# DeltaNet's convolution and SiLU in a Trainium2 encoder step: per group of 384 tokens at the eviction of the projection, in place of per tile of 128 in the DeltaNet stage

## Chip, cores and metric

One Trainium2 chip, one NeuronCore of it. The metric is device time of one launch in microseconds (us). Times per instruction come from one profiled execution.

## What is computed

One layer of a streaming encoder for 2048 prompt tokens and 8 x 16 sample tokens (2176 tokens, 17 tiles of 128). One input projection feeds three token mixers: chunked band attention, gated DeltaNet, and an S5 state-space model (S5). Their outputs go through an output projection, a layer norm, a feed-forward network (FFN) and a second layer norm. The part that the change concerns is the head of DeltaNet:

```
buf = concat([conv_buf, qkv_b], axis=1)          # 3 earlier rows, then the projected 768 columns
new_conv = buf[:, -3:]
conv = depthwise causal convolution of width 4 over buf (768 channels)
conv = silu(conv + b_conv_b)
qb, kb, vb = split(conv, 3)
qb, kb = l2_normalize(qb), l2_normalize(kb)
ob, s_new = gated_delta_rule(qb, kb, vb, g, beta, s0)
```

For the prompt `conv_buf` is zero before the first token; for the 8 sample streams it is an input of 3 rows each.

## The kernel before

All features lie on partitions: the 768 q/k/v channels of DeltaNet are 6 blocks of 128 channels, called f = 0 to 5 here.

**Projection.** `project1` goes through the tokens in three parts of 768, 768 and 640 tokens, each part in two groups (384 and 384; in the last part 384 and 256, the 256 being 128 prompt tokens and the 128 sample tokens). For every part `feat` is called with blocks of 256 output columns: first S5's input, then `tok` for value columns and gates, then three `feat` calls for the q/k/v channels of DeltaNet, then one for DeltaNet's output gate. One `feat` call makes four PSUM tiles (2 halves of 128 columns x 2 groups), each from 8 x 3 matmuls, since a product of fp32 numbers is made of three products of split parts. The PSUM pool for them, `pp`, has 2 buffers. Each PSUM tile is evicted by ScalarE (`evac`, L198) into a tile of the pool `st` (2 buffers, `to_rows`), which SyncE's DMA queue (SP) then stores to the DRAM buffer `bT[part]`. `project2` and `project2_all` make the attention's q, k and v in the same way afterwards.

**DeltaNet.** `deltanet` takes the 17 tiles in pairs (0 1, 2 3, ... 10 11, then the sample tile 16, then 12 13, 14 15). `b_pre` loads a tile's six blocks from `bT` with three earlier columns (`cin`, 3 buffers, L499 to L505), and for each block does: on ScalarE the first tap with the bias (L510), on VectorE three taps (L512), on ScalarE a tanh (L514), on VectorE the closing product (L515; silu(x) is x(1 + tanh(x/2)) up to a factor that the later scales hold). The result `s2` (1 buffer) is transposed by TensorE (L528, L535). `b_inverse` inverts the 16x16 diagonal blocks on VectorE (L625, L627) with a round trip through DRAM, `b_solve` and `b_rec` are chains of small matmuls (L649, L686 to L694) and VectorE steps, `b_out` ends the tile.

**Order.** The two streams are Python generators. Part 0 is projected alone; from then on the emission alternates between DeltaNet and the projection of parts 1 and 2, and later between DeltaNet, `project2_all` and `s5`. A list scheduler then fixes the order in which each engine, and each DMA queue, gets its instructions. At run time an engine takes them strictly in that order, so an instruction that waits holds everything behind it on its engine. After this stage come attention, the output projection and the FFN.

## Time and profile before

| | us |
|---|---|
| median of 3 runs (2867.49 to 2869.89) | 2867.68 |
| the profiled execution, own time | 2862.88 |
| its span | 2861.1 |
| TensorE (PE) busy in the span | 2739.1 |
| VectorE (DVE) busy | 1945.7 |
| ScalarE (ACT) busy | 1316.4 |
| GpSimd (POOL) busy | 1096.7 |

In the rows below, PE is the matmul part of TensorE and PEld its weight loads. L512 is line 512 of the kernel before. "out<-in" names the tile that is written and the tiles that are read. "idle before" is the idle time of the engine just in front of an instruction, with what ended it. The chain of waits is followed back from the last instruction: at each step to what released it, or to the instruction in front of it on its engine.

### The profile page before, as it was taken

How to read it: one execution, taken by the hardware profiler on the slowest of the kernel's cores; microseconds unless marked ns; L12 is line 12 of the kernel's file. 1: busy time of each engine (PE TensorE's matmuls, PEld its weight loads, DVE VectorE, ACT ScalarE, POOL GpSimd, SP SyncE). 2: the span in 40 equal slices, each digit the busy share in tenths (PEclk: the TensorE clock that was granted, in tenths of full speed). 3: DMA queues.
4: the chain of work that ended last, by engine and by line, in shares of the span. 5: the costliest groups of instructions: out<-in, count | busy, mean ns of one | idle time of the engine just before them, and what ended most of it. 6: DMA issues, size and time to landing. Idle time of an engine off the chain costs nothing.

```text
span 2861.1 us, 46393 instructions
## 1 busy us (share of the span) xinstructions
PE 2739.1 (96%) x16685; PEld 2404.6 (84%) x16685; DVE 1945.7 (68%) x4908; ACT 1316.4 (46%) x2743; POOL 1096.7 (38%) x972
## 2 busy tenths in 40 slices
PE   8999999989989899999999999999999999999998
PEld 8988888867677677788889989979999898888897
DVE  7587888798653788778755555566665656566666
ACT  3554554343355778612334334354344345444443
POOL 0011111231221223002654444465555554677674
PEclk9999999999999999999999999999999999999999
DMA  5644445455457651244612212252222225322321
GB/s 184 208 107 119 115 121 127 137 150 151 152 156 247 204 160 57 92 148 162 240 63 80 68 60 74 74 206 104 74 89 89 74 79 201 112 89 89 118 83 58
DMA packets 292429, 351.89 MB, mean 123 GB/s; under 512 B 85586, under 2 KB 218534, under 8 KB 291878
## 3 DMA queue, kind: packets, MB, share of 16 engines
q1 hardware_dynamic: 292198, 348.92, 38.9%
q8 instruction: 131, 2.15, 0.3%
q14 instruction: 100, 0.82, 0.1%
HBM read 276.58 MB, written 74.89 MB: 123 GB/s over the span
## 4 chain that ended last, share of the span: by engine, by line
PE 70%; DVE 12%; POOL 5%; DMA 5%; ACT 4%; issue 4%; SPq 1%; DVEq 0%; ACTq 0%; POOLq 0%
PE fdp L66 7%; PE fdp L65 7%; PE fdp L67 7%; PE pps L66 3%; PE pps L67 3%; PE pps L65 3%; PE wops L66 2%; PE wops L65 2%; PE wops L67 2%; PE fupv L65 2%; PE fupv L66 2%; PE fupv L67 2%; PE fupz L67 2%; PE bqs L649 2%; PE fupz L66 2%
## 5 line engine op out<-in xcount | busy, mean ns | idle before, releaser
L1552 POOL TENSOR_TENSOR wu<-wur,wu 128x512 fp32r<-128x512 f32 x315 | 424.2, 1350 | 530.8 <-ACT wu L1551 512.2
L1670 DVE TENSOR_TENSOR fy<-fy,fdp 128x512 f32<-128x512 f32 x500 | 342.3, 687 | 271.8 <-PE fdp L67 270.2
L1551 ACT CAST wu<-wur 128x512 fp32r<-128x512 f32 x315 | 194.0, 617 | 450.8 <-DMA wur<-in_w_upL 203.5
L65 PE MATMUL fdp<-wdh,hh 128*128 128x512 f32 x1020 | 397.8, 390 | 2.4 <-DVE fy L1670 1.9
L66 PE MATMUL fdp<-wdl,hh 128*128 128x512 f32 x1020 | 397.3, 389 | 0.0
L67 PE MATMUL fdp<-wdh,hl 128*128 128x512 f32 x1020 | 397.1, 389 | 0.0
L65 PE MATMUL pps<-xh,wh 128*128 128x384 f32 (+2 forms) x800 | 279.5, 351 | 12.4 <-ACT xh L60 10.6
L66 PE MATMUL pps<-xl,wh 128*128 128x384 f32 (+2 forms) x800 | 279.6, 349 | 2.1 <-DVE xl L61 2.0
L67 PE MATMUL pps<-xh,wl 128*128 128x384 f32 (+2 forms) x800 | 277.4, 347 | 0.1
L65 PEld LDWEIGHTS fdp<-wdh,hh 128*128 128x128 f32 x1020 | 191.5, 188 | 42.5 <-DVE fy L1670 3.7
L1617 DVE TENSOR_TENSOR hl<-fre,hh 128x384 fp32r<-128x384 f32 (+1 forms) x180 | 162.9, 906 | 92.1 <-ACT hh L1616 91.3
L67 PEld LDWEIGHTS fdp<-wdh,hl 128*128 128x128 f32 x1020 | 191.5, 188 | 39.9
L66 PEld LDWEIGHTS fdp<-wdl,hh 128*128 128x128 f32 x1020 | 191.5, 188 | 38.0 <-DVE wdl L61 0.2
L60 ACT CAST wdh<-wdr 128x1024 fp32r<-128x1024 f32 x94 | 97.9, 1050 | 174.2 <-PE fdp L67 171.0
L65 PEld LDWEIGHTS pps<-xh,wh 128*128 128x128 f32 x800 | 152.0, 191 | 24.7 <-ACT xh L60 12.1
L61 DVE TENSOR_TENSOR wl<-wr,wh 128x512 fp32r<-128x512 f32 (+1 forms) x152 | 107.5, 716 | 87.8 <-ACT wh L60 80.1
L66 PEld LDWEIGHTS pps<-xl,wh 128*128 128x128 f32 x800 | 151.8, 190 | 14.0 <-DVE xl L61 5.3
L67 PEld LDWEIGHTS pps<-xh,wl 128*128 128x128 f32 x800 | 151.7, 190 | 11.4 <-issue 1.8
L61 DVE TENSOR_TENSOR wdl<-wdr,wdh 128x1024 fp32r<-128x1024 f32 x94 | 143.7, 1536 | 10.6 <-ACT wdh L60 10.5
L60 ACT CAST wh<-wr 128x512 fp32r<-128x512 f32 (+1 forms) x152 | 92.6, 619 | 81.7 <-DMA wr<-in_w_inA 35.4
L1612 ACT ACTIVATE fre<-fre,ld_b_up 128x384 f32<-128x384 f32 (+1 forms) x144 | 86.0, 597 | 87.4 <-DVE fre L1621 61.9
L1229 ACT ACTIVATE P<-P,st 128x640 f32<-128x640 f32 (+4 forms) x128 | 97.2, 760 | 30.6 <-DVE st L1226 29.8
(559 smaller groups left out, 7268.5 us busy)
## 6 DMA issues: line engine op xcount, KB each, us to landing
wdr<-in_w_dnL SPq DMA_DIRECT2D x96, 512.0 KB
wur<-in_w_upL SPq DMA_DIRECT2D x92, 512.0 KB
wr<-in_w_inA SPq DMA_DIRECT2D x70, 512.0 KB
TU<-tD SPq DMA_DIRECT2D x34, 256.0 KB
y<-in_x SPq DMA_DIRECT2D x17, 512.0 KB
x<-y SPq DMA_DIRECT2D x17, 512.0 KB
fxr<-x SPq DMA_DIRECT2D x17, 512.0 KB
fy<-x SPq DMA_DIRECT2D x17, 512.0 KB
```

Source lines behind the costliest of these rows:

```text
L60: nc.scalar.copy(hi, src)
L61: nc.vector.tensor_tensor(lo, src, hi.bitcast(F32), OP.subtract)
L65: mm(out, lh, rh, start=first, stop=False, **kw)
L66: mm(out, lh, rl, start=False, stop=False, **kw)
L67: mm(out, ll, rh, start=False, stop=last, **kw)
L649: mm(ps[:, h * n:(h + 1) * n], lhs[:, h], rhs[:, h], start=True, stop=True)
L1229: self.nc.scalar.activation(x, x, AF.Exp, scale=-1.0, bias=st[:, q:q + 1], accum_out=st[:, 2 + q:3 + q])
L1551: self.nc.scalar.copy(hi, src)
L1552: P.tensor_tensor(lo, src, hi.bitcast(F32), OP.subtract)
L1612: nc.scalar.activation(r, src, AF.Relu, bias=self.bu[:, c * 2 + i:c * 2 + i + 1])
L1617: V.tensor_tensor(hl, r, hh.bitcast(F32), OP.subtract)
L1670: V.tensor_tensor(y, y, ps[x], OP.add)
```

## The change

The convolution and SiLU move from `b_pre` into a new function `c_group`, called for each PSUM tile of the three q/k/v `feat` calls in place of `to_rows`. `evac` now writes into `cx` (2 buffers), which has three columns more; GpSimd copies the last three columns of the group before from `ch` into it (L329) and the last three new ones back to `ch` (L331). The taps then run over the whole group (384 columns; in the last part's second group over 128 prompt and 128 sample columns apart, with the streams' own three columns, L335). `bT` now holds the result, stored from `co`, which takes a buffer of `st`; the tanh takes a buffer of `xr` (6 buffers, until now only for loads of x). `b_pre` loads all six blocks of a tile with one DMA into `s2` (L525). The weights and history of the convolution are loaded at the start of `project1` instead of in `b_consts`.

```diff
--- before.py
+++ after.py
@@ -270,6 +270,7 @@
 
         up = [upp.tile([128, 16, NC5], F32, name=f"up{m}") for m in range(2)]
         self.p_pools(es, 1)
+        self.c_setup(upp)
         for j, (t0, T, groups) in enumerate(PARTS):
             w = self.weights(A["w_inA"][0])
             x = self.load_x(t0, groups)
@@ -291,15 +292,54 @@
             self.tok(A["w_inG"], 264, x, groups, keep_v)
             yield 2
             for i in range(3):
-                self.feat(1 + i, x, groups, self.to_rows(self.bT[j], i * 256, 0, groups))
+                self.feat(1 + i, x, groups, lambda m, z, ps: self.c_group(j, 2 * i + m, groups[z], ps))
                 yield 2
             self.feat(8, x, groups, self.to_rows(self.gT[j], 0, 0, groups), by_group=True)
             yield 2
             if j == 2:
+                nc.sync.dma_start(A["o_cvp"], self.ch)
+                nc.sync.dma_start(A["o_cvs"], self.cvs)
                 yield from self.project2(3, x, groups)
         for m in range(2):
             for g in range(8):
                 nc.sync.dma_start(self.uS[m * 8 + g].rearrange("(s h) c -> h s c", h=16), up[m][g * 16:g * 16 + 16])
+
+    def c_setup(self, pool):
+
+        self.cp_ = pool
+        self.cw, self.cb, self.hist = self.ld(pool, "b_cw"), self.ld(pool, "b_cb"), self.ld(pool, "b_hist")
+        self.ch = pool.tile([128, 6, 3], F32, name="ch")
+        self.nc.gpsimd.memset(self.ch, 0.0)
+        self.cvs = pool.tile([128, 6, 8, 3], F32, name="cvs")
+
+    def c_group(self, j, f, group, ps):
+
+        nc = self.nc
+        V = nc.vector
+        n0, n = group
+        m = min(n, SEQ - PARTS[j][0] - n0)
+        o = self.st_p.tile([128, n], F32, name="co", tag="st")
+
+        def conv(o, x):
+            nc.scalar.activation(o, x[0], AF.Identity, scale=self.cw[:, f, 0:1], bias=self.cb[:, f:f + 1])
+            for k in range(1, 4):
+                V.scalar_tensor_tensor(o, x[k], self.cw[:, f, k:k + 1], o, OP.mult, OP.add)
+
+        x = self.cp_.tile([128, m + 3], F32, name="cx", tag="cx", bufs=2)
+        nc.gpsimd.tensor_copy(x[:, 0:3], self.ch[:, f])
+        self.evac(x[:, 3:], ps[:, 0:m])
+        nc.gpsimd.tensor_copy(self.ch[:, f], x[:, m:m + 3])
+        conv(o[:, 0:m], [x[:, k:k + m] for k in range(4)])
+        if m < n:
+            x = self.cp_.tile([128, 8, 19], F32, name="cxs", tag="cxs", bufs=1)
+            nc.gpsimd.tensor_copy(x[:, :, 0:3], self.hist[:, f])
+            self.evac(x[:, :, 3:], ps[:, m:n].rearrange("p (b t) -> p b t", t=16))
+            nc.gpsimd.tensor_copy(self.cvs[:, f], x[:, :, 16:19])
+            conv(o[:, m:n].rearrange("p (b t) -> p b t", t=16), [x[:, :, k:k + 16] for k in range(4)])
+        th = self.xr_p.tile([128, n], F32, name="cth", tag="xr")
+        nc.scalar.activation(th, o, AF.Tanh, scale=0.5)
+        V.scalar_tensor_tensor(o, th, 1.0, o, OP.add, OP.mult)
+        nc.sync.dma_start(self.bT[j][f * 128:(f + 1) * 128, n0:n0 + n], o)
 
     def project2(self, j, x, groups):
 
@@ -372,9 +412,8 @@
         self.sel, self.sel16 = self.ld(c, "c_sel"), self.ld(c, "c_sel16")
         self.mtri, self.mtri16, self.moff = self.ld(c, "c_mtri"), self.ld(c, "c_mtri16"), self.ld(c, "c_moff")
         self.id16 = self.ld(c, "c_id16")
-        self.cw, self.cb, self.nw = self.ld(c, "b_cw"), self.ld(c, "b_cb"), self.ld(c, "b_nw")
+        self.nw = self.ld(c, "b_nw")
         self.nea, self.dtb = self.ld(c, "b_alog"), self.ld(c, "b_dtb")
-        self.hist = self.ld(c, "b_hist")
         self.ones = c.tile([128, 128], F32, name="ones")
         V.memset(self.ones, 1.0)
         V.tensor_scalar(self.nw, self.nw, 0.5, None, OP.mult)
@@ -483,40 +522,7 @@
         c0 = ps0 * 128
         src = self.bT[pj]
         s2 = bw.tile([128, 6, T], F32, name="s2", tag="s2")
-        cv = bw.tile([128, 6, 8 if sam else 1, 3], F32, name="cv", tag="cv")
-        for f in range(6):
-            fr = slice(f * 128, (f + 1) * 128)
-            if sam:
-                cin = bw.tile([128, 8, 19], F32, name="cins", tag="cin", bufs=3)
-                nc.sync.dma_start(cin[:, :, 3:19], src[fr, c0:c0 + T].rearrange("p (b t) -> p b t", t=16))
-                nc.gpsimd.tensor_copy(cin[:, :, 0:3], self.hist[:, f])
-                nc.gpsimd.tensor_copy(cv[:, f], cin[:, :, 16:19])
-                xin = [cin[:, :, k:k + 16] for k in range(4)]
-                o = s2[:, f].rearrange("p (b t) -> p b t", t=16)
-            else:
-                cin = bw.tile([128, T + 3], F32, name="cin", tag="cin", bufs=3)
-                if t0 == 0:
-                    nc.gpsimd.memset(cin[:, 0:3], 0.0)
-                    nc.sync.dma_start(cin[:, 3:], src[fr, 0:T])
-                elif c0 == 0:
-                    nc.sync.dma_start(cin[:, 0:3], self.bT[pj - 1][fr, 765:768])
-                    nc.sync.dma_start(cin[:, 3:], src[fr, 0:T])
-                else:
-                    nc.sync.dma_start(cin, src[fr, c0 - 3:c0 + T])
-                if t0 + n == 16:
-                    nc.gpsimd.tensor_copy(cv[:, f, 0], cin[:, T:T + 3])
-                xin = [cin[:, k:k + T] for k in range(4)]
-                o = s2[:, f]
-            nc.scalar.activation(o, xin[0], AF.Identity, scale=self.cw[:, f, 0:1], bias=self.cb[:, f:f + 1])
-            for k in range(1, 4):
-                V.scalar_tensor_tensor(o, xin[k], self.cw[:, f, k:k + 1], o, OP.mult, OP.add)
-            th = bw.tile([128, T], F32, name="th", tag="th", bufs=2)
-            nc.scalar.activation(th, s2[:, f], AF.Tanh, scale=0.5)
-            V.scalar_tensor_tensor(s2[:, f], th, 1.0, s2[:, f], OP.add, OP.mult)
-        if sam:
-            nc.sync.dma_start(A["o_cvs"], cv)
-        elif t0 + n == 16:
-            nc.sync.dma_start(A["o_cvp"], cv[:, :, 0])
+        nc.sync.dma_start(s2, src[:, c0:c0 + T].rearrange("(f p) t -> p f t", p=128))
         qk = bw.tile([128, n, 8, 64], F32, name="qk", tag="qk", bufs=2)
         ss = bw.tile([128, n * 8], F32, name="ss", tag="ss", bufs=2)
         R = []
```

VectorE, where `b_pre` of tile 13 is followed by tile 14's. Before, from `qkn` of tile 13 on; `s_8708` is `s2` of tile 14, `ZC` belongs to S5, `F`, `kdec`, `at` and `qkT` to tile 13:

```order
L572 TENSOR_TENSOR qkn<-qk,F 128x512
L548 TENSOR_TENSOR F<-F,b_egc 128x4
L577 TENSOR_TENSOR kdec<-qk,F 128x256
L515 SCALAR_TENSOR_TENSOR s_8708<-th,s_8708 128x128
L512 SCALAR_TENSOR_TENSOR s_8708<-cin,ld_b_cw,s_8708 128x128 x6
L956 TENSOR_TENSOR ZC<-ld_s_x1c,prs 128x272
L515 SCALAR_TENSOR_TENSOR s_8708<-th,s_8708 128x128
L603 TENSOR_TENSOR at<-bps,DT 128x2x64
L603 TENSOR_TENSOR qkT<-bps,DM 128x2x64
L603 TENSOR_TENSOR at<-bps,DT 128x2x64
L603 TENSOR_TENSOR qkT<-bps,DM 128x2x64
L515 SCALAR_TENSOR_TENSOR s_8708<-th,s_8708 128x128
```

The same place in the changed kernel, from `qkn` of tile 13 (now L578) on (`tp` and `Ti` are the inverse, of tiles 12 and 13):

```order
L578 TENSOR_TENSOR qkn<-qk,F 128x512
L554 TENSOR_TENSOR F<-F,b_egc 128x4
L583 TENSOR_TENSOR kdec<-qk,F 128x256
L609 TENSOR_TENSOR at<-bps,DT 128x2x64
L609 TENSOR_TENSOR qkT<-bps,DM 128x2x64
L609 TENSOR_TENSOR at<-bps,DT 128x2x64
L609 TENSOR_TENSOR qkT<-bps,DM 128x2x64
L631 TENSOR_TENSOR tp<-blk,Ti 64x15
L633 TENSOR_TENSOR Ti<-Ti,tp 64x15
L631 TENSOR_TENSOR tp<-blk,Ti 64x28
L633 TENSOR_TENSOR Ti<-Ti,tp 64x14x2
L631 TENSOR_TENSOR tp<-blk,Ti 64x39
```

Between `kdec` and the products `at` and `qkT` (L603, now L609), and behind them, there is no instruction of the convolution any more; the inverse follows at once.

GpSimd, in part 1 of the projection, around the products of tile 2. Before (`qdkb`, `R`, `DM` and `at` are made in `b_pre`, `osq` in `b_out`):

```order
L608 TENSOR_TENSOR at<-at,ld_c_moff 128x256
L570 TENSOR_TENSOR DM<-DT,ld_c_mtri 128x256
L574 TENSOR_TENSOR qdkb<-qk,F 128x512
L575 TENSOR_TENSOR R<-qk,F 128x4x64
L770 TENSOR_TENSOR osq<-o 128x256
L608 TENSOR_TENSOR at<-at,ld_c_moff 128x256
```

The same stretch in the changed kernel:

```order
L331 COPY ch<-cx 128x3
L329 COPY cx<-ch 128x3
L331 COPY ch<-cx 128x3
L329 COPY cx<-ch 128x3
L580 TENSOR_TENSOR qdkb<-qk,F 128x512
L581 TENSOR_TENSOR R<-qk,F 128x4x64
L329 COPY cx<-ch 128x3
L614 TENSOR_TENSOR at<-at,ld_c_moff 128x256
L576 TENSOR_TENSOR DM<-DT,ld_c_mtri 128x256
L776 TENSOR_TENSOR osq<-o 128x256
L331 COPY ch<-cx 128x3 x2
```

The copies of the carried columns (`cx<-ch` in front of a group's convolution, `ch<-cx` behind its eviction) now stand between those steps of DeltaNet.

SP, from the first instruction on. Before:

```order
L71 DMA ld_c_ident<-in_c_ident 128x128
L210 DMA wr<-in_w_inA 128x1024 x2
L225 DMA xr<-in_xT 128x384 x6
```

In the changed kernel:

```order
L71 DMA ld_c_ident<-in_c_ident 128x128
L71 DMA ld_b_cw<-in_b_cw 128x24
L71 DMA ld_b_cb<-in_b_cb 128x6
L71 DMA ld_b_hist<-in_b_hist 128x144
L210 DMA wr<-in_w_inA 128x1024 x2
L225 DMA xr<-in_xT 128x384 x6
```

Three small loads moved in front of the first weights of the projection (`wr`).

## Rows read from the trace of the kernel before

**Rows 1.** The page: span, busy time and share of each engine.
```profile
span 2861.1 us, 46393 instructions
PE 2739.1 (96%) x16685; PEld 2404.6 (84%) x16685; DVE 1945.7 (68%) x4908; ACT 1316.4 (46%) x2743; POOL 1096.7 (38%) x972
```
**Rows 2.** Busy time of each engine in five stretches (us from the start).
```profile
0.00:100.00 100.00, 89.95 (x544) 88.64 (x545) 62.57 (x255) 36.79 (x75) 1.76 (x10) 1.00 0.65 199
100.00:430.00 330.00, 319.29 (x2387) 287.20 (x2387) 268.41 (x1076) 176.64 (x455) 46.75 (x53) 1.00 0.46 126
430.00:585.00 155.00, 149.97 (x1150) 130.56 (x1148) 118.21 (x446) 61.37 (x158) 34.71 (x71) 1.00 0.47 126
585.00:625.00 40.00, 29.41 (x169) 23.44 (x169) 37.32 (x128) 19.27 (x45) 16.41 (x23) 0.83 0.59 165
625.00:760.00 135.00, 127.89 (x857) 101.63 (x856) 107.99 (x343) 48.22 (x108) 28.79 (x45) 0.99 0.50 144
```
**Rows 3.** L512 (a tap) alone in two stretches: DVE busy, count, clock, DMA.
```profile
100.00:430.00 330.00, 68.48 (x199) 1.00 0.46 126
430.00:760.00 330.00, 36.66 (x105) 0.97 0.50 138
```
**Rows 4.** Chain of waits by line, first 100 to 430, then 430 to 760 us.
```profile
by line: issue 10.8%; PE pps L67 10.1%; PE pps L66 10.1%; PE pps L65 9.9%; PE bqs L649 8.1%; DVE s L512 4.9%; PE brs L692 2.7%; PE brs L690 2.6%; DMA cin<-bT 2.4%; PE brs L694 2.3%; PE brs L686 2.2%; DVE tp L625 2.1%; DVE Ti L627 2.0%; PE b
...
by line: PE bqs L649 7.8%; PE pps L66 7.1%; PE pps L67 7.1%; PE pps L65 7.0%; issue 5.3%; DVE s L512 4.8%; PE brs L692 3.2%; PE brs L690 3.1%; PE brs L736 2.8%; PE brs L694 2.7%; PE brs L686 2.7%; DVE Ti L627 2.4%; DVE Sst L699 2.0%; DVE tp
```
**Rows 5.** Chain of waits, in order of time, 586 to 608 us.
```profile
586.46 0.51 ACT sq L531
...
595.26 1.93 DVE s L512 x6
...
604.07 0.48 PE bps L535
...
607.53 0.85 PE pps L67 x2
```
**Rows 6.** PE's waits from 100 to 760 us: total, times, longest.
```profile
PE bps L535 <- DVE s L515: 5.4, 3, 4.5
```
**Rows 7.** DVE timeline, back to back: start, length, instructions.
```profile
104.64 1.96 DVE L61 TENSOR_TENSOR xl<-xr,xh 128x384 fp32r<-128x384 f32 x4
...
186.08 1.65 DVE L512 SCALAR_TENSOR_TENSOR s<-cin,ld_b_cw,s 128x128 f32<-128x128 f32 x6
...
188.41 0.49 DVE L515 SCALAR_TENSOR_TENSOR s<-th,s 128x128 f32<-128x128 f32 x2
```
**Rows 8.** Tile `cin`: its loads, as SP issues them.
```profile
L505 SPq DMA_DIRECT2D cin<-bT x78: 319/364/868, 111.7 to 640.3; - x78
L502 SPq DMA_DIRECT2D cin<-bT x12: 319/372/435, 256.3 to 511.2; - x12
L503 SPq DMA_DIRECT2D cin<-bT x12: 422/435/1191, 256.6 to 511.7; - x12
```
**Rows 9.** Chain of waits, two of its first pieces.
```profile
0.74 0.40 SPq L71
...
1.65 5.36 DMA wr<-in_w_inA
```
**Rows 10.** ACT timeline: an eviction, and the idle time since the one before it.
```profile
67.52 0.49 ACT L198 ACTIVATE st<-pps 128x384 f32<-128x384 f32 x1 [3.70 <-PE pps L67]
```
**Rows 11.** GpSimd's waits from 100 to 760 us: total, times, longest.
```profile
POOL qdkb L574 <- DVE F L549: 101.2, 9, 31.0
POOL osq L770 <- ACT o L702: 86.7, 15, 15.9
```
**Rows 12.** ACT groups by shape: the first tap, the tanh, the eviction.
```profile
L510 ACT ACTIVATE s<-cin,ld_b_cb,ld_b_cw 128x128 f32<-128x128 f32 x96 | 43.8, 488 | 12.0 <-DMA cin<-bT 7.3 <-PE bps L535 4.4
L514 ACT ACTIVATE th<-s 128x128 f32<-128x128 f32 x102 | 31.2, 310 | 65.5 <-DVE s L512 53.8 <-DVE ons L348 2.2 <-DVE F L546 1.8
L198 ACT ACTIVATE st<-pps 128x384 f32<-128x384 f32 x48 | 23.3, 488 | 48.5 <-PE pps L67 44.7 <-issue 3.3 <-ACT s L510 0.3
```

## The prediction

> **What bounds the kernel now.** Read the page first: TensorE (PE) is busy 96% of the span and VectorE 68% [rows 1]. The change touches only the stage in which the projection and DeltaNet run beside each other, so next come the windows of that stage [rows 2]. PE is busy 90 of the first 100 us, 319 of the 330 us from 100 to 430, 150 of 155 up to 585, then only 29.4 of 40 us, then 128 of 135. VectorE is busy 268 of 330 and 37.3 of 40 us in the same windows. A busy PE is not a full one: where a small matmul waits for another engine, its latency counts as busy. So the third view is the chain of waits [rows 4]: from 100 to 430 us the taps of the convolution (L512) are 4.9% of it and the loads of `cin` 2.4%; from 430 to 760 us the taps are 4.8%. That is 16.2, 7.9 and 15.8 us of 330. The place where it shows best is 586 to 608 us [rows 5]: between the last square of one tile and the transposes of the next (L535) the chain runs through six taps in a row, and the matmuls behind it go slowly (0.85 us for two). The granted clock of 585 to 625 us is 0.83 [rows 2]: full level outside and half level (1.2 GHz) for (1 - 0.83) x 2 x 40 = 13.6 us, after PE had stood still; half of that, 6.8 us, is lost.
>
> **The change, part by part.** The sum is made against the profiled execution (2862.88 us, span 2861.1).
>
> *Work on VectorE.* Back to back, a tap of 128 columns takes (1.65 - 0.34)/5 = 0.26 us and the closing product 0.21; a 384-wide operation of two tensors takes (1.96 - 0.55)/3 = 0.47 [rows 7]. The 384-wide tap isn't in the trace: at least 0.47, at most three small ones, 0.79; I take 0.47 + 0.05 = 0.52, since the small tap lies 0.05 above the small product and both differ from it only in the operand that scales. A tile costs 18 x 0.26 + 6 x 0.21 = 5.9 us now, 17 tiles 101 us. Afterwards 30 full groups cost 3 x 0.52 + 0.47 = 2.0 us each and 6 split ones (two times 128 columns) some 6 x 0.26 + 0.34 = 1.9: 72 us. Of these, 12 groups (24 us) fall in the first 100 us, beside 37 idle us of VectorE; 24 groups (48 us) fall between 100 and 430 us, where 199 taps, so 11 tiles or 65 us, are gone; and nothing is left after 430, where 105 taps or 6 tiles, 35 us, are gone [rows 2, 3].
>
> *Work on ScalarE.* The first tap (0.49) and the tanh (0.31) go 102 times and come back 36 times and a little, three times as wide; the eviction stays [rows 12]. ScalarE is busy 177 of 330 us and less later [rows 2], so this is costed at nothing; without that cover it would be a gain as well.
>
> *DMA.* 108 loads of `cin` (102 for prompt and borders [rows 8], 6 for the samples) become 17 of 384 KB. A load takes 0.32 to 0.44 us of SP's queue, so some 35 us of issue go. How long the new load lands isn't in the trace; 512 KB took 5.4 us [rows 9], so between nothing and that. `s2` has one buffer, so it starts when the six transposes of the tile before are done, in place of a convolution that takes at least 5.9 us from the same point: no loss.
>
> *Start.* Three small loads stand in front of the first weights on SP, each some 0.40 us, and the first weights are the head of the chain [rows 9]: +1.2 us.
>
> *Part 0 of the projection.* PE makes a PSUM tile in 0.49 + 3.70 = 4.2 us [rows 10]. An eviction now needs a `cx` buffer, free only when the taps of two groups before are done, and the stores stand behind the convolution in SP's queue with weight loads behind them. VectorE is still building S5's tables there. Between 0 and 6 us; I take +1, since two PSUM tiles and two `cx` buffers give four groups, 17 us, for a chain of some 4 us.
>
> *100 to 430 us.* 24.1 us of the chain are taps and `cin`. Three quarters of the VectorE work is still in the stretch, but no longer between a tile's load and its transposes; what is late next is the inverse and the small matmuls of the solve, all on the chain already. Between 0 and -24; I take a third, -8.
>
> *585 to 625 us.* PE is idle 10.6 us and loses 6.8 to the clock: at most -17.4. VectorE has only 0.26 x 20 or so of taps in its 37 busy us, so S5's and DeltaNet's own steps are late next. I take -11, near the idle time, since the taps stand in front of just the transposes that PE waited for [rows 5, 6].
>
> *The rest of 430 to 760 us.* Of 15.8 us of taps on the chain some 5 are in the 40 us above; of the other 11 I take -7, since nothing comes back there.
>
> Sum: 1.2 + 1 - 8 - 11 - 7 = -24 us, so 2839 for a profiled execution. The median of the runs lies 4.8 us above the profiled one, and the same step from it gives **2844**. The stages after 760 us keep their order and move as a whole.
>
> *A rule that speaks against it.* The Trainium skill, Perfetto Trace Analysis, Optimizing Scalar/DVE Operations, says that where such an engine isn't saturated but makes bubbles on others, smaller instructions may let work finish sooner; here 384 columns replace 128 on an engine that is busy 81% in that stretch [rows 2]. What that would give is rival C. The trace bears it out only in part, since VectorE was at 93% in the 40 us where PE stood still.
>
> **Rivals.**
>
> *A, PE is the bound.* For it: 97% busy from 100 to 430 us, and its order hardly moves. Then only PE's direct waits on the closing product go, 5.4 us [rows 6], and 2.2 come at the start: 2862.9 - 3.2, with the median at 2864. Against it: the PE lines listed make up only half of the chain there [rows 4].
>
> *B, slower: the carried columns tie the projection to DeltaNet.* GpSimd takes the copies in order, between steps that it waits for: 101 us in 9 waits for a factor of b_pre and 87 us in 15 for the output of the recurrence, so 6 to 11 us each [rows 11]. A copy behind such a step holds the group's first tap, that holds ScalarE, and two groups later the eviction and PE. It decides from the point where the wait is longer than the two PSUM tiles in hand, 8.4 us. If a third of the 24 interleaved groups lose one tile's 4.2 us, that is +34, the -8 is lost as well, and the sum is -24 + 8 + 34 = +18: 2886. Against it: the steps waited for stand in PE's own queue in front of most of these groups, and most waits are shorter than 8.4 us.
>
> *C, wide instructions hold small ones.* 24 x 4 operations between 100 and 430 us are 0.26 us longer than before; if each holds a step of the chain for that long, +25 eats the gain: 2869.
>
> *D, all of it comes off the chain.* -24 - 17 - 11 + 1.2 = -51: 2817. For it: the chain counts only what ended last. Against it: what is late next is close, since VectorE is 76 to 93% busy.
>
> That the change doesn't do what it says can be left out, except that the last group of each block stays at 128 columns, which is in the sum.
>
> **Chances.** The forecast 0.54, D 0.19, A 0.08, C 0.06, B 0.13. A measurement of this kernel tells a change of 0.2% (5.7 us) from none. The forecast, D and half of A are faster: 0.77; half of A and C the same: 0.10; B slower: 0.13. The range for 8 in 10: at its low end it reaches nearly to D's whole price, 2820, at its high end to C, 2869, past A; B lies outside, with the last bit of D.
>
> **What would show it.** In the profile of the changed kernel: 246 fewer instructions on VectorE (408 of the convolution become 162), 120 fewer on ScalarE, and none of the convolution after some 430 us; no hole of PE and no fallen clock around 585 us, and DeltaNet's last steps some 20 us earlier; taps on 384 columns at 0.5 to 0.6 us back to back. The forecast is wrong if PE's waits for the eviction of projection tiles come up in the first 430 us (B), if the chain there keeps its length with wide taps in it (C), or if the gain is there but the stage after 760 us gives it back through another transfer.

## The result and the profile after

The changed kernel takes 2886.6 us (median of 6 runs, 2881.5 to 2893.8) against 2869.6 us of the kernel before on the same chip: a ratio of 1.0063 [1.0049, 1.0077], 17 us slower. The profiled execution took 2890.3 us; the two profiled spans lie 27 us apart, so some 10 us of what the traces show is the difference between single executions.

The page of the changed kernel, against [rows 1]:

```profile
span 2888.3 us, 45898 instructions
PE 2749.7 (95%) x16685; PEld 2412.3 (84%) x16685; DVE 1931.8 (67%) x4662; ACT 1290.0 (45%) x2623; POOL 1122.2 (39%) x1033
```

VectorE lost the forecast 246 instructions, ScalarE 120. The windows, with the columns of [rows 2] and one stretch more:

```profile
0.00:100.00 100.00, 87.66 (x517) 84.98 (x518) 78.52 (x281) 43.59 (x87) 11.49 (x31) 1.00 0.58 176
100.00:430.00 330.00, 317.14 (x2372) 285.82 (x2370) 251.96 (x883) 160.59 (x379) 66.57 (x108) 1.00 0.45 128
430.00:585.00 155.00, 144.09 (x1059) 125.19 (x1058) 103.89 (x382) 47.35 (x115) 30.21 (x60) 0.97 0.45 128
585.00:625.00 40.00, 31.49 (x242) 27.23 (x240) 28.20 (x109) 16.61 (x37) 12.62 (x16) 0.89 0.43 121
625.00:760.00 135.00, 127.24 (x840) 101.44 (x838) 100.58 (x308) 40.03 (x84) 29.81 (x42) 0.96 0.49 139
760.00:920.00 160.00, 139.54 (x702) 113.32 (x701) 87.73 (x183) 76.28 (x154) 30.27 (x32) 0.96 0.59 181
```

VectorE is relieved from 100 us on (252 in place of 268 us of 330, then 104 in place of 118 of 155), and PE is no fuller for it: 317 in place of 319, then 144 in place of 150. Its granted clock, which had fallen mainly in the 40 us around 600 (0.83; 0.99 from 625 to 760 us), now lies at 0.89 to 0.97 in four stretches.

Where the time went shows best when PE's work is counted: every group of matmuls gets its usual start-to-start time (the tenth percentile of its form over these kernels), and the table says when the kernel before had done so much of that work (us), and how far behind it each other kernel is at the same work. e1 to e10 are experiments, told below. The count is an estimate: the kernels do the small and the dense matmuls in different orders, and with the median of each form as its price the same traces give lags of the changed kernel and of e1 that differ from the table by up to 2.5 us (7.5 in place of 8.6 for the changed kernel at 382.6, 17.6 in place of 19.5 at 580.9, 15.7 in place of 14.0 at 649.7). A step of under some 3 us isn't shown by it. The last dense matmul of the stage starts at 915 us before and at 941 us after.

```
work   before  after    e1     e4     e10    e7     e8
  40     52.9    1.1   1.1    1.9    1.4   -0.2    1.1
  80     94.8    4.5   1.3    3.0    2.5   -0.5    0.4
 200    236.1    4.1  -1.2    9.4    5.6    6.1    3.6
 320    382.6    8.6   1.6    9.8    5.3   15.5   20.6
 360    430.7   15.9   1.2    9.0    7.2   36.1   25.1
 440    530.0   15.2  -0.7   11.8    7.0   53.3   25.1
 480    580.9   19.5   4.6   12.5    8.6   55.5   25.8
 520    649.7   14.0  -1.1   11.3    2.8   67.0   20.4
 600    749.4   16.2  -1.3    9.5    3.1   70.3   21.9
 720    904.9   24.4   4.7    7.3    3.2   71.9   19.8
```

The chain of waits from 430 to 760 us has lost the taps [rows 4], with the dense matmuls at 20% of it, as before (21%):

```profile
by line: PE bqs L655 9.5%; issue 9.2%; PE pps L65 6.7%; PE pps L67 6.5%; PE pps L66 6.5%; PE brs L698 2.9%; PE brs L696 2.9%; PE brs L742 2.8%; PE brs L700 2.5%; PE brs L692 2.3%; DVE Ti L633 2.3%; DVE wl L61 2.3%; DVE Sst L705 1.8%; POOL q
```

PE's waits from 100 to 760 us (total, times, longest), where [rows 6] had the closing product:

```profile
PE brs L792 <- DVE osq L781: 9.1, 5, 4.3
PE pps L67 <- DVE wl L61: 6.2, 3, 3.9
PE pps L65 <- ACT wh L60: 5.7, 1, 5.7
```

And GpSimd's, whose waits for DeltaNet are those of [rows 11], while nothing but 1.6 us of PE's waits is for `cx`:

```profile
POOL qdkb L580 <- DVE F L555: 99.0, 11, 37.3
POOL osq L776 <- ACT o L708: 88.0, 12, 16.2
```

The lag comes in four steps: 4.5 us by the end of part 0, 7 us around 435 us, 4 us around 560, and 8 us after 750; around 600 some 2 to 5 us come back. The rise around 560 and the fall around 600 stand in the column of e1 too, which has no convolution. The step at 435 us in PE's timeline:

```profile
434.45 0.34 PE L66 MATMUL pps<-xl,wh 128*128 128x384 f32 x1
436.57 0.44 PE L792 MATMUL brs<-ld_c_ident,osq 128*128 128x128 f32 x2 [1.78 <-DVE osq L781]
440.89 0.69 PE L67 MATMUL pps<-xh,wl 128*128 128x384 f32 x1 [3.88 <-DVE wl L61]
```

PE waits for `osq` of a DeltaNet tile, then for `wl`, the low part of the next block's weights. What VectorE did in that time:

```profile
435.10 0.34 DVE L326 SCALAR_TENSOR_TENSOR co<-cx,ld_b_cw,co 128x128 f32<-128x128 f32 x1
...
435.64 0.33 DVE L326 SCALAR_TENSOR_TENSOR co<-cxs,ld_b_cw,co 128x128 f32<-128x128 f32 x1
...
436.11 0.41 DVE L781 TENSOR_TENSOR osq<-o,onz 128x256 f32<-128x256 f32 x1
...
438.08 0.34 DVE L326 SCALAR_TENSOR_TENSOR co<-cxs,ld_b_cw,co 128x128 f32<-128x128 f32 x1
...
439.19 0.41 DVE L341 SCALAR_TENSOR_TENSOR co<-cth,co 128x256 f32<-128x256 f32 x1
...
440.16 0.68 DVE L61 TENSOR_TENSOR wl<-wr,wh 128x512 fp32r<-128x512 f32 x1
```

The taps and closing products of the last groups of part 2 stand in VectorE's queue in front of both. Behind the hole the clock falls:

```profile
430.00:440.00 10.00, 5.23 (x36) 4.67 (x34) 9.94 (x48) 4.97 (x12) 1.13 (x3) 0.95 0.53 122
440.00:450.00 10.00, 9.02 (x67) 8.31 (x67) 7.89 (x35) 2.25 (x5) 2.15 (x2) 0.71 0.66 178
```

0.71 is half level (1.2 GHz) for a good half of those 10 us. Summed over windows of 10 us up to 1000 us, the missing share of the clock is 27 us after and 17 us before: up to 10 of the 27 us between the two profiles.

### The profile page after: what moved, and what is told of

The parts are those of the page before. It is cut to its first block, busy times and chain, and to the rows that moved or that the text cites. A ratio compares the mean times of both kernels' runs of the same rounds, so it can differ in the third digit from the quotient of the medians.

```text
span 2888.3 us, 45898 instructions
## 1 busy us (share of the span) xinstructions
PE 2749.7 (95%) x16685; PEld 2412.3 (84%) x16685; DVE 1931.8 (67%) x4662; ACT 1290.0 (45%) x2623; POOL 1122.2 (39%) x1033
## 4 chain that ended last, share of the span: by engine, by line
PE 64%; DVE 9%; POOL 6%; DMA 5%; ACT 4%; issue 3%; SPq 1%; DVEq 0%; ACTq 0%; POOLq 0%
PE fdp L66 7%; PE fdp L67 7%; PE fdp L65 7%; PE wops L66 2%; PE wops L65 2%; PE wops L67 2%; PE bqs L655 2%; PE pps L65 2%; PE fupv L65 2%; PE pps L66 2%; PE fupv L66 2%; PE pps L67 2%; PE fupz L67 2%; PE fupv L67 2%; POOL wu L1558 2%
```

## Experiments

All ratios are to the kernel before, run on the same chip in the same series; its median lay between 2865.0 and 2868.6 us in these.

**e1, no convolution at all.**

```diff
...
-        conv(o[:, 0:m], [x[:, k:k + m] for k in range(4)])
...
+        self.evac(o, ps)
```

> Leaves out the convolution, SiLU and the carried columns altogether: the group goes from its eviction straight to the store, DeltaNet gets the raw projection. It gives the price of everything that the convolution costs at its new place. Theory T (the taps and closing products stand in VectorE's order in front of steps that PE waits for, as the hole at 434 to 441 us shows), theory S (the stores wait on SP for the closing product, with weight loads behind them) and theory B (the carried columns on GpSimd tie the projection to DeltaNet) all expect 2845 to 2862 us. If the convolution bounded nothing at its old place either (rival A of the prediction), a kernel without any convolution stays at 2860 to 2870, no faster than the kernel before. By the prediction's own sum it would lie at 2840 or lower.

Measured: 2874.6 us, 1.0037 [1.0025, 1.0049], above every theory's number. VectorE is busy 1868.0 us in place of the 1945.7 before, so 78 us less (the prediction had counted 101 us back to back), and the kernel is 10 us slower than before, not faster, and 8 us faster than the changed one (2874.6 against 1.0063 x 2865 = 2883). In PE's work it stays within 5 us of the kernel before all along, and up to 749 us it is level with it (-1.3). So what the prediction hoped to gain at the old place isn't there. What the convolution costs at its new place is 8 us by the ratios and 17 us by the table up to 749 us (16.2 against -1.3): behind that point e1 loses 6 us of its own, at a split that the last section shows. Two of e1's waits from 585 to 780 us (engine, line, waited for: us, times, longest), both behind loads and splits of x and weights:

```profile
PE pps L66 <- DVE xl L61: 8.0, 4, 6.2
PE pps L65 <- ACT wh L60: 6.2, 1, 6.2
```

**e2, carried columns on ScalarE.**

```diff
-        nc.gpsimd.tensor_copy(x[:, 0:3], self.ch[:, f])
+        nc.scalar.copy(x[:, 0:3], self.ch[:, f])
...
```

> The four small copies of carried columns per group go from GpSimd to ScalarE, which makes the eviction itself; nothing else changes. Theory B: the tie to GpSimd's queue is gone, 2860 us or less, at least half of the 17 us comes back. Theories T and S: GpSimd was never waited for (PE waited 1.6 us for cx in the whole stage), so 2882 to 2892, within 5 us of the changed kernel; the copies on ScalarE cost at most 0.2 us each.

Measured: 2882.4 us, 1.0052 [1.0032, 1.0072], each of the two ratios within the other's interval. Theory B, which wanted at least half of the 17 us back, falls. It is rival B of the prediction, which had named 2886 us, almost the measured time: the number was right by luck and the mechanism wrong.

**e3, stores of the convolved groups from GpSimd's queue.**

```diff
-        nc.sync.dma_start(self.bT[j][f * 128:(f + 1) * 128, n0:n0 + n], o)
+        nc.gpsimd.dma_start(self.bT[j][f * 128:(f + 1) * 128, n0:n0 + n], o)
```

> The store of each convolved group is issued from GpSimd's queue in place of SP's, so that no weight or x load stands behind a store that waits for the closing product (SP waited some 98 us for such stores in the changed kernel). Theory S: 2865 to 2875 us. Theory T: weights were loaded in time and only split late, so 2883 to 2890. Theory B: slower than the changed kernel, since GpSimd waits longer, 2890 or more.

Measured: 2897.3 us, 1.011 [1.0095, 1.0125], 14 us worse than the changed kernel. Theory S's number fails, but the run doesn't settle S, since it makes a new wait. GpSimd's from 50 to 450 us, then PE's up to 460 us:

```profile
POOL bT L342 <- DVE co L341: 21.0, 14, 3.4
```
```profile
PE pps L65 <- ACT cx L198: 6.5, 3, 3.0
```

Now it is GpSimd's queue, with the carried columns in it, that waits for the closing product, and PE waits 6.5 us for the eviction into `cx`, in the changed kernel 1.6. The Trainium skill, Perfetto Trace Analysis, DMA Optimizations, suggests giving loads to one engine's queue and stores to another's; here that cost 14 us, and the other queue held copies that the next eviction needs.

**e4, the taps one group later.** `c_flush(1)` writes the taps, tanh, closing product and store of all waiting groups but the last.

```diff
...
+        self.pend.append((j, f, n0, n, m, x, xs))
+        self.c_flush(1)
```

> The taps, tanh, closing product and store of a group are written one group later (3 buffers of cx, 4 of xr), and after the next weight block's splits where a new block begins, so that VectorE gets the splits of the last weights, and the closing step of a DeltaNet tile, ahead of the last taps. Theory T: the hole of PE at 434 to 441 us (6 us, and some 3 us of clock behind it) goes, 2872 to 2880 us, and PE no longer waits there for wl. Theories S and B: the stores and the carried columns come no earlier, 2884 to 2892.

Measured: 2872.5 us, 1.0028 [1.0016, 1.004]: 10 us come back. VectorE at the same place (L348 is a tap there, L795 `osq`):

```profile
432.64 0.67 DVE L61 TENSOR_TENSOR wl<-wr,wh 128x512 fp32r<-128x512 f32 x1
...
439.05 0.41 DVE L795 TENSOR_TENSOR osq<-o,onz 128x256 f32<-128x256 f32 x1
...
440.60 0.68 DVE L61 TENSOR_TENSOR wl<-wr,wh 128x512 fp32r<-128x512 f32 x1
...
441.68 0.33 DVE L348 SCALAR_TENSOR_TENSOR co<-cx,ld_b_cw,co 128x128 f32<-128x128 f32 x1
```

The splits come ahead of the last taps, PE waits 0.7 us for `osq` there, for `wl` not at all, and the column e4 has no step at 430 us. Theory S, for which e4 should have stayed at 2884 or more, fails here. The taps are as wide as before, so these 10 us came from their place and not from their width: rival C's rule that smaller instructions let work finish sooner (the Trainium skill, Perfetto Trace Analysis, Optimizing Scalar/DVE Operations) isn't what decided here; narrower taps at the new place weren't tried.

**e9, its control: the buffers of e4, the taps at once.**

```diff
-        x = self.cp_.tile([128, m + 3], F32, name="cx", tag="cx", bufs=2)
+        x = self.cp_.tile([128, m + 3], F32, name="cx", tag="cx", bufs=3)
...
-        self.xr_p = self.pool(f"xr{n}", 6 if n == 1 else 2, es=es)
+        self.xr_p = self.pool(f"xr{n}", 4 if n == 1 else 2, es=es)
```

> The changed kernel with the buffers of e4 (3 of cx, 4 of xr) and without its later place of the taps: the control for e4. Theory T (the place of the taps in VectorE's order is what counts): as the changed kernel, 2881 to 2892 us, with the waits for wl and osq around 435 us still there. If the third cx buffer did it in e4: 2878 or less.

Measured: 2887.7 us, 1.007 [1.0057, 1.0082], as the changed kernel. With e4 this shows that the place of the taps in the order is worth 10 to 12 us. Not all of that is the hole at 435 us: in the table e4 lies 5 us behind the changed kernel at 236 us, 7 ahead of it at 431 and 749, and 17 ahead at 905.

**e5, the kernel before without its convolution.**

```diff
-        for f in range(6):
...
+        nc.sync.dma_start(s2, src[:, c0:c0 + T].rearrange("(f p) t -> p f t", p=128))
...
```

> The kernel before with the convolution and SiLU left out of b_pre (a tile loads its six raw blocks with one DMA and goes on); projection, constants and pools stay as they were. The price of the convolution at its old place. The prediction's sum: 24 to 42 us, so 2823 to 2841. Theory A (its work lay beside other waits that end no earlier: weights, x, DeltaNet's own steps): within 6 us of the kernel before, 2859 to 2871. e1, which differs from this one by the three loads of constants at the start and the place of tiles in SBUF alone, took 2874.6; if this one takes as long, its 10 us come from the order that the scheduler makes without a convolution, if it takes 2865 they come from the start.

Measured: 2885.0 us, 1.0061 [1.0044, 1.0077], outside both theories. It does the same work as e1 and takes 7 us more; at 105 us alone, where PE waits 4.5 us for an eviction by ScalarE, it falls some 6 us behind. So kernels of equal work lie several us apart here by order and place alone. That it is no faster agrees with e1. Both kernels without a convolution lose some us at the same point of S5; e5's PE from 750 to 800 us (e1's row is the first of the two above):

```profile
PE pps L66 <- DVE xl L61: 6.9, 2, 6.0
```

**e6 and e15, only the constants loaded first**, at the start of `project1` in place of `b_consts`; e15 has `self.s5c` for `upp`.

```diff
         self.p_pools(es, 1)
+        self.cw, self.cb, self.hist = self.ld(upp, "b_cw"), self.ld(upp, "b_cb"), self.ld(upp, "b_hist")
...
```

> The kernel before with nothing changed but the place of the three loads of the convolution's constants (ahead of the first weights, as in the changed kernel). The prediction's term: +1.2 us, 2866 to 2867. If the order that the scheduler makes is itself worth several us whatever the work (theory N), it may move by 3 to 8 us to either side.

Measured: 2889.2 us, 1.0076 [1.0059, 1.0092], 22 us for three small loads. In its trace the first cast of x for `project2_all` comes at 646 us, directly behind the last first tap of the convolution (before: at 600 us), and five loads of x that wait for it at 649 us (before: by 616); ScalarE, then SP:

```profile
641.17 0.88 ACT L510 ACTIVATE s<-cin,ld_b_cb,ld_b_cw 128x128 f32<-128x128 f32 x2
...
645.73 1.12 ACT L60 CAST xh<-xr 128x512 fp32r<-128x512 f32 x2
```
```profile
648.71 10.30 SPq L225 DMA_DIRECT2D xr<-in_xT x5
```

The constants stood in a pool whose memory `project2_all` takes over. Hence e15, where they stand in a pool that lasts:

> e6 again, with the constants in a pool that lasts through the whole stage, so that no x tile of project2_all waits for their memory. If the 22 us of e6 are that wait (x loads at 649 in place of 592 us): the prediction's +1.2 us remains, 2866 to 2871. Theory N (any shift of the order costs several us): 2874 or more.

Measured: 2869.6 us, 1.0007 [0.9995, 1.0019]. The 22 us were that memory; the start itself costs what was forecast (0.9 us at 53 us), and this shift of the order costs at most 5 us.

**e7, each tap of the kernel before twice.**

```diff
-            for k in range(1, 4):
+            for k in (1, 2, 3, 1, 2, 3):
```

> The kernel before with each of the three taps of a block done twice (another result, 306 taps or some 80 us of VectorE more, in the same place). The prediction's view, in which taps at the old place stood on the chain at about a quarter of their length: +20 us or more, 2885 or above. Theory A, if the cover is deep: under 6 us, 2871 or less. Between them: the cover is used up by the first set of taps.

Measured: 2936.6 us, 1.0244 [1.0229, 1.0259]: 70 us, and VectorE is busy 2014.2 us in place of 1945.7, so 69 us more. No theory had this with e1: one set of taps is free, a second costs its whole length.

**e8, part 0 by tile, parts 1 and 2 as in e4.**

```diff
+        if j == 0:
+            st = self.st_p.tile([128, n], F32, name="st", tag="st")
+            self.evac(st, ps)
...
+            return
```

> As e4 (one group later), but part 0 of the projection stores its groups raw and tiles 0 to 5 are convolved in b_pre as before (2 buffers of cin, 1 of th); parts 1 and 2 are convolved at the eviction. In e4 all of the lag against the kernel before (8.4 us) had come up by the start of part 1 of the projection at 120 us. Theory L (the loss of e4 is the convolution beside part 0, where PE has nothing but dense matmuls to do and VectorE still makes S5's tables): 2864 to 2868. If the old place costs what the prediction said, tiles 0 to 5 bring some 8 us back: 2872 to 2876.

Measured: 2891.5 us, 1.0087 [1.0072, 1.0103], outside both. Its lag is 0.4 us at the end of part 0, where theory L is right, and 25 us at 430, nearly all of it from 236 us on. The taps of tiles 0 to 5 (98.6 to 279.3 us) lie beside those of parts 1 and 2; but VectorE is no busier for it than before, so why these 21 us are lost stays open. PE and VectorE from 235 to 430 us, in the kernel before and in e8 (columns as in the windows above):

```profile
235.00:430.00 195.00, 189.68 (x1458) 167.40 (x1457) 160.51 (x666) 100.08 (x259) 27.91 (x30) 1.00 0.46 120
```
```profile
235.00:430.00 195.00, 179.62 (x1365) 158.73 (x1364) 154.64 (x607) 93.55 (x230) 36.51 (x62) 0.97 0.44 119
```

**e10, e11, e12 and e18, towards a version that beats both.** e10 is e4 with

```diff
-            th = self.xr_p.tile([128, n], F32, name="cth", tag="xr")
+            nc.scalar.activation(x[:, 0:m], o[:, 0:m], AF.Tanh, scale=0.5)
...
```

so that the tanh lies in `cx`, with 5 buffers of `xr`, and the constants loaded after the first x. e11 also raises the buffers of x in `project2_all` from 2 to 4, e12 does that alone to the kernel before; e18 is e10 with `st` of 3 and `xr` of 4 buffers.

> As e4, but the tanh goes into cx itself, so that xr (5 buffers) serves loads of x alone, and the three constants are loaded after the first weights and x. Counted in PE's work, e4 lay 9.4 us behind the kernel before at 137 us and 7 to 11 us ever after. If that lag is the start (1.1 us) and the x loads of part 1 that wait for slots which hold tanhs, most of it goes: 2863 to 2868, level with the kernel before. If it is the taps beside S5's tables in part 0, 2870 to 2873. Theory P (the old place cost 24 us): 2850 or less.

> As e10, with 4 buffers in place of 2 for the x loads of project2_all. If PE's hole where project2_all begins (6 us in the changed kernel and in e1, 10 us in e4, ended by the splits of weights and x) comes from x loads that wait for a buffer: 3 to 8 us below e10. If it comes from where the loads stand in SP's order, behind the last evictions: within 3 us of e10.

> The kernel before with nothing changed but 4 buffers in place of 2 for the x loads of project2_all: the control for e11. The waits for xl where project2_all begins are 2.5 us in the kernel before, so at most that much: 2863 to 2868. If a shift of the order alone is worth several us (theory N, which e6 did not decide, since there the constants held memory that the x tiles of project2_all needed): 3 to 10 us to either side.

> e10 with a third buffer of st (for it xr has 4 in place of 5). In part 0 of the changed kernel ScalarE's first tap waits 7.5 us in three times for the store of co to land, since co holds one of two buffers of st until then, and the next eviction stands behind it. If that is what remains of part 0's loss (e10 lies 2.5 us behind the kernel before at 95 us): 2 to 4 us below e10, level with the kernel before or a little faster, 2862 to 2867. If x loads with one buffer less take it back, or the stores were not it: 2868 to 2872.

Measured: e10 2869.4 us, 1.0013 [1.0003, 1.0023]; e11 2869.5, 1.0011 [1.0002, 1.002]; e12 2868.6, 1.0009 [1, 1.0018]; e18 2872.4, 1.0019 [1.0008, 1.003]. e10 lies 2 to 8 us below e4 from 236 us on; the start is 0.5 us of it, the rest fits the x loads that shared slots with the tanh, which weren't tried apart from the fifth buffer. More x buffers change nothing (e11), so the hole where `project2_all` begins isn't theirs, and e18's third store buffer, paid with one of x, gives nothing. None beats the kernel before.

**e13, e14, e16, e17: less work for PE.** In the q, k, v projection one of three products is left out.

```diff
-                self.mm3(ps[:, :n], w[k][0][:, ms], w[k][1][:, ms], *x[k, z], k == 0, k == 7)
+                if two:
+                    self.nc.tensor.matmul(ps[:, :n], w[k][0][:, ms], x[k, z][0], start=k == 0, stop=False)
+                    self.nc.tensor.matmul(ps[:, :n], w[k][0][:, ms], x[k, z][1], start=False, stop=k == 7)
...
```

> The kernel before with one of the three products left out (another result) in the projection of the q, k and v channels: 48 us of PE's work less (288 matmuls less; 240 of 384 columns at 0.175 us and 48 of 256 at 0.12), 17 us of it in part 0 and 31 beside DeltaNet; VectorE's work is the same. Theory PE (PE and the latencies in its order bound the stage, with VectorE's taps under them): 40 to 48 us less, 2818 to 2826. Theory V (VectorE is the bound, as e7 suggests): only part 0's 17 us and little else, 2842 to 2850. Theory K (both stand at the same limit, so that taking work from either alone gives little): between them, 2826 to 2842.

> e1 (no convolution at all) with the same 48 us of PE's work left out. Theory PE: as far below e1 as e13 lies below the kernel before, 2826 to 2834, not faster than e13. Theory K: with VectorE relieved PE's whole 48 us come off, 2826 to 2832, and e14 is at least 8 us faster than e13. Theory V: faster than e13 by 25 us or more.

Measured: e13 2869.7 us, 1.0004 [0.9995, 1.0014]; e14 2837.1 us, 0.9883 [0.9868, 0.9898]. Taking 48 us from PE alone gives nothing, taking the convolution alone gives nothing (e1), taking both gives 31 us. The windows from 100 to 430 us in e13, then in e14:

```profile
100.00:430.00 330.00, 292.08 (x2169) 257.75 (x2167) 267.65 (x1087) 174.90 (x452) 53.37 (x55) 0.95 0.48 128
```
```profile
100.00:430.00 330.00, 313.07 (x2388) 278.58 (x2388) 226.37 (x867) 141.18 (x337) 49.13 (x54) 0.99 0.50 141
```

With less work PE idles (busy 292 of 330 us) while VectorE still has its 268; counted in PE's work, e13 falls behind e14 only between 253 and 406 us, by 34 us, and keeps that. The largest hole is at 287 to 302 us, where PE is busy 3.3 of 15 us and VectorE 14.4. PE's longest single wait from 235 to 430 us:

```profile
PE bps L587 <- DVE F L552: 7.3, 1, 7.3
```

Some of the 34 us is the clock, which the theories hadn't counted: from 253 to 406 us it is 0.92 in e13, where it fell to half level (1.2 GHz) in that hole, and 1.00 in e14, so 12 us of clock are missing, and they cost something only where PE has work. Up to 1000 us the missing share is 46 us in e13, 27 in e14 and 17 in the kernel before, so at most 29 of the 48 us that PE was spared went there. e13's number fits none of the three theories, which had all given it something; that only both together pay speaks for K's idea of two limits near each other, but how much of e13's loss is VectorE and how much the clock behind it isn't separated. Then the change itself:

> The changed kernel with the 48 us of PE's work of e13 left out (same other result as e13). Theory K (PE and the chain through VectorE are two limits of equal length; the change shortens the second one only): with PE shortened too, the changed kernel is faster than e13 by 10 to 25 us, 2845 to 2860, where with all of PE's work it was 17 us slower. If the convolution at the eviction is itself the new limit: 2870 or more, no faster than e13.

> e10 (taps one group later, tanh in cx) with the same work of PE left out. Theory K: 10 to 17 us below e16, as e10 is below the changed kernel, and above e14 (2837), which has no convolution: 2838 to 2850.

Measured: e16 2872.4 us, 1.0023 [1.0012, 1.0035]; e17 2866.3, 1.0007 [0.9997, 1.0017]. K's numbers fail here. Against e14, e16 is 15 us behind by the end of part 0 and some 30 from 352 us on; up to 1000 us its clock misses 41 us and e17's 51, against e14's 27, so part of this too may be the clock. In part 0 the clock can't be it (7 us missing in e16 up to 100 us, 3 in e14): there the convolution at the eviction is a limit as well once PE is shorter. PE's wait for evictions up to 120 us in e16 (5.7 us in e14):

```profile
PE pps L242 <- ACT cx L198: 17.1, 5, 8.1
```

ScalarE's wait in part 0 (50 to 110 us), first in the changed kernel, then in e16, is for the store of `co` to land, with the next eviction behind it:

```profile
ACT co L324 <- DMA bT<-co: 7.5, 3, 4.1
```
```profile
ACT co L328 <- DMA bT<-co: 11.1, 3, 6.7
```

## Why the prediction was wrong

**What bounds the kernel: this step failed.** The prediction took the taps' share of the chain of waits [rows 4] for a price, a third of it from 100 to 430 us and most of it later, and gave rival A, PE as the bound, 8 in 100. The chain names what ended last; it doesn't say how far behind the next one was. e1 does: with no convolution at all the kernel is level with the one before at 749 us, so the terms of -8, -11 and -7 had nothing to take. PE's own stream, 319 of 330 us busy [rows 2], lies close behind the one through VectorE; e13 and e14 agree, with the clock as an open share. For the gains alone rival A's 2864 us would have been near. It doesn't follow that VectorE had room at its old place: a second set of taps there cost its whole length (e7).

**Start, +1.2.** Right: 1.1 us at 53 us of the table, and e15 shows the same alone.

**Part 0, +1 (0 to 6).** 4.5 - 1.1 = 3.4 us, inside its bounds. The prediction counted `cx` and PSUM buffers. PE waits there only 1.6 us for evictions and 1.1 us for a split (50 to 130 us; before: 0.4 us in all). Behind the evictions ScalarE waits 7.5 us for `co`, which holds one of two `st` buffers until its store has landed. That this is the whole loss isn't shown: with a third buffer (e18) ScalarE waits 2.3 us for it, in e10 3.1, and no time is gained.

**100 to 430 us, -8.** From 4.5 us at 95 to 8.6 us at 383: no gain, and none in e1 (1.3 to 1.6 us), where the taps are gone altogether.

**585 to 625 us, -11.** At most half: the lag falls by 5.5 us (19.5 to 14.0), by 2 with the median prices, and 4 us of that had come up just before, around 560. From 530 to 650 us together it falls by 1 us (15.2 to 14.0), in e1 by 0.4. The hole behind the taps [rows 5, 6] is gone, and another stands at the same place of the program; the changed kernel's PE, ScalarE and SP:

```profile
614.05 0.38 PE L541 MATMUL bps<-ld_c_ident,s 128*128 128x128 f32 x2
620.09 0.79 PE L65 MATMUL pps<-xh,wh 128*128 128x512 f32 x1 [5.65 <-ACT wh L60]
```
```profile
619.42 1.14 ACT L60 CAST wh<-wr 128x512 fp32r<-128x512 f32 x2 [1.32 <-DMA wr<-in_w_inA]
```
```profile
614.23 0.32 SPq L249 DMA_DIRECT2D qT<-st  x1
614.60 0.43 SPq L225 DMA_DIRECT2D xr<-in_xT  x1
615.12 0.87 SPq L210 DMA_DIRECT2D wr<-in_w_inA  x2
```

The first weights of `project2_all` are issued at 615 us, behind the last store of an eviction, when PE already waits. Before, they were issued from 597 us on, while PE waited for the taps. The prediction had named S5's steps as late next, not these loads.

**Rest of 430 to 760 us, -7.** Wrong in sign: from 383 to 581 us the lag grows by 11 us. 7 of them come at 435 us, where the convolution's last groups stand in front of `osq` and the weights' splits; the 4 around 560 can't be that, since the last convolution ends at 440 us and e1 has them too. "Nothing comes back there" overlooked that moved work is put in front of something on its new place's queues; the prediction asked what waits for SP and GpSimd, and not for VectorE and ScalarE. e4 and e9 show it for the step at 435 us.

**After 760 us, moved as a whole.** Wrong: 8 us more (16.2 to 24.4). PE's order there hardly differs; its waits for splits of x and for S5 differ, and the clock is 0.83 in four windows of 10 us (before: 0.66 in one). e4 and e10 don't have it; e1 loses 6 us there, at the split of the last section. Which of the earlier shifts makes it wasn't tried.

**The details held:** taps of 384 columns back to back at (2.20 - 0.61)/3 = 0.53 us (0.61 is one alone), the last convolution ending at 439.6 us.

```profile
84.49 2.20 DVE L326 SCALAR_TENSOR_TENSOR co<-cx,ld_b_cw,co 128x384 f32<-128x384 f32 x4
```

## What to carry to other kernels

A share of the chain of waits is no price: before counting on it, leave the work out altogether, then take work from the engine that stands beside it, then from both; here only both together paid. Look at the granted clock of each such run, since TensorE, when it is made to wait, may lose to the clock what it was spared (e13). Work that is moved goes in front of something at its new place: list, for each engine it lands on, what stands behind it at the changes of blocks (splits of the next weights, a closing step that PE waits for), and write it one step later if the next weights would wait. A tile that takes over memory waits for its last reader, so a constant's pool counts as much as the time of its load (22 us in e6).

## Not expected of the hardware

In e1 PE waited 6.15 us for a split of x at 764 us. Four instructions of VectorE in front of that split took some three times as long as elsewhere (1.78 us in place of 0.68, 1.39 in place of 0.42) while GpSimd ran the products for `kst`, 4.1 us more in sum, so they are the larger part of the wait. VectorE, then GpSimd:

```profile
759.75 0.67 DVE L61 TENSOR_TENSOR xl<-xr,xh 128x512 fp32r<-128x512 f32 x1
...
761.74 1.78 DVE L61 TENSOR_TENSOR wl<-wr,wh 128x512 fp32r<-128x512 f32 x1
...
767.60 1.39 DVE L1000 TENSOR_TENSOR sB<-sZ,tab 64x256 f32<-64x256 f32 x1
```
```profile
759.88 1.09 POOL L946 TENSOR_TENSOR tz<-ld_s_x2c,pi 128x272 f32<-128x272 f32 x1 [1.83 <-DVE Kt L967]
...
761.68 2.98 POOL L1173 TENSOR_TENSOR kst<-kr,kst 64x512 fp32r<-64x512 f32 x2
765.92 2.79 POOL L1173 TENSOR_TENSOR kst<-kr,kst 64x512 fp32r<-64x512 f32 x2 [1.25 <-ACT kst L1172]
```

The split at 759.75 takes its usual 0.67 us beside the product for `tz`, the one at 761.74 takes 1.78 beside that for `kst`. What differs is which of the two began first: the first split began 0.13 us ahead of `tz`, and it is `tz` that took longer, 1.09 us against a median of 0.68. Where the split comes second it is slow beside `tz` too; the kernel before, VectorE, then GpSimd:

```profile
600.61 1.21 DVE L61 TENSOR_TENSOR xl<-xr,xh 128x512 fp32r<-128x512 f32 x1 [0.50 <-ACT xh L60]
```
```profile
599.73 1.54 POOL L957 TENSOR_TENSOR tz<-ld_s_x2c,pi 128x272 f32<-128x272 f32 x2 [3.31 <-issue]
```

In e1's trace up to 1000 us the 11 splits of 128x512 that began ahead of the GpSimd instruction beside them took 0.67 to 0.69 us; of those that began behind it, some took up to 1.78. The Trainium skill, GPSIMD Engine Reference, Specifications, says that GpSimd's access to SBUF is shared with VectorE and contends with instructions of two SBUF inputs; the trace agrees, for `kst` and for `tz`.
